# Three heads of an HGRN2 mixer project two token blocks by Strassen's seven products, and the mixers' outputs pass through DRAM

## The chip, the cores and the metric

The kernel runs on one core of one Trainium2 chip. Its time is the device time of an execution in microseconds, as the median of several runs. TensorE (PE) multiplies into PSUM banks, its matmuls preceded by loads of weights (PEld); VectorE (DVE), ScalarE (ACT) and GpSimd (POOL) do the element-wise work; DMAs are issued from SyncE's queue (SP). Each engine works through its own queue in order and waits at an instruction whose operands or buffers are not ready.

## What is computed

One inference step of a hybrid layer on 1056 tokens (1024 of a prompt, 32 of eight running sequences), all in float32 with a width of 1024. Cut to what matters:

```python
h = _rmsnorm(x, norm_mix)
p = jnp.einsum('btd,dp->btp', h, w_in) + b_in
qk_a, v_a, o_a, i_a, f_a, q_b, f_b, i_b, g_b = jnp.split(p, offs, axis=-1)
out_a = _mlstm_mixer(...)            # 4 heads of 128
out_b = _hgrn_mixer(q_b, f_b, i_b, g_b, S0, lb, hgrn_norm)   # 4 heads of 128
#   f = lb + (1 - lb) * sigmoid(f_raw);  k = (1 - lb) * sigmoid(-f_raw);  q = silu(q_raw)
#   chunks of 64: gated linear attention with a state S;  out = headnorm(o) * silu(g_raw)
x = x + concat([out_a, out_b]) @ w_out
h2 = _rmsnorm(x, norm_ffn)
x = x + (silu(h2 @ w_gate) * (h2 @ w_up)) @ w_down
```

The states of both mixers are outputs too.

## The kernel before, in words

Everything lies transposed: features on the 128 partitions, tokens along a row. The tokens form three blocks: block 0 of 288 (256 of the prompt and the 32 samples), blocks 1 and 2 of 384. A float32 operand is split into a rounded part (HI, whi) and the rest (LO, wlo), both in a format that TensorE multiplies fast, and a product is three matmuls: hi x hi, hi x lo, lo x hi (lines 135 to 137). ScalarE makes the rounded part and GpSimd the rest (lines 96 and 97).

The work is a list of units, in the order of TensorE. A unit is one weight tile (128 outputs by 1024 inputs) against one block: 8 steps along the inputs of 3 matmuls, 24 in all, into a PSUM bank, which an evacuation then empties. First come the four heads of the mLSTM mixer, then from unit 51 the four heads of HGRN2, each with tiles for f, q, v and g and three blocks, so 12 units a head; then the output projection and the feed-forward part, which already works by Strassen's scheme.

Between the matmuls of a unit stand hooks, one after every 6 matmuls. At a hook each active generator takes its next step: the mixers (`mix_b` for HGRN2), the splitting of weight tiles (`split`), the norms. A mixer of one head and block takes some 32 hooks, so two or three overlap: products of 16 or 32 columns on TensorE (line 775), merging by masked copies (line 782), state updates (line 899), steps that multiply halves of the queries and keys by gates (lines 794, 796 and 802) with copies on ScalarE (lines 799 and 800), the gate product of a new mixer on GpSimd (line 804). Its result goes into X in place (line 928), in the place that the normalised input has left.

Weight tiles come through two raw buffers; when a tile is split, the load for the tile after next is issued. `next_splits` starts a split eight units ahead of the first use, or as soon as one of five split buffers is free. The projections' banks come from three buffers named mm; the evacuations are lines 472 and 474 (v, q, g) and 741 to 744 (f and the key made of it). On SP's queue the DMAs stand in the order in which they were written.

Of the kernel before, what the change touches and what calls it, by code (L numbers as in the profile page):

```python
# [16 lines left out]
T = 1056  # L17
# [23 lines left out]
def hybrid_step(ctx: ExitStack, tc: tile.TileContext, i, o):  # L41
# [13 lines left out]
    units, tiles = [], []  # L55
# [30 lines left out]
    def split(t, pool):  # L86
# [11 lines left out]
        if t < NRAW:  # L98
            load(t + 4)
        elif 4 <= t and t + NRAW < len(tiles) and (t + NRAW < n_t1) == (t < n_t1):  # L100
            load(t + NRAW)
# [19 lines left out]
    def unit(t, rhs, nk, evac, stride=128, coff=0, post=None, tag="mm"):  # L121
        units.append(dict(t=t, rhs=rhs, nk=nk, evac=evac, stride=stride, coff=coff, post=post, tag=tag))

    def emit_k(u, ks):
# [3 lines left out]
        if ks[0] == 0:  # L128
            u["ps"] = bank(u["tag"])
        ps = u["ps"]  # L130
        hi, lo = his[t], los[t]
        for k in ks:
            c = k * u["stride"] + u["coff"]
            wh, wl = hi[:, c:c + 128], lo[:, c:c + 128]
            nc.tensor.matmul(ps[:, :n], wh, rh[:, k, :], start=(k == 0), stop=False)  # L135
            nc.tensor.matmul(ps[:, :n], wh, rl[:, k, :], start=False, stop=False)  # L136
            nc.tensor.matmul(ps[:, :n], wl, rh[:, k, :], start=False, stop=(k == nk - 1))  # L137
# [24 lines left out]
    def mo(b):  # L162
        return X[:, :, PO[b]:PO[b] + NPR[b]]
# [74 lines left out]
    def tl(tag, n=384, bufs=2, dt=F32, p=128):  # L238
        return mp.tile([p, n], dt, tag=tag, name=tag, bufs=bufs)
# [34 lines left out]
    d_x = dram.tile([128, KT, T], F32, name="d_x")  # L274
    d_h = dram.tile([128, KT, T], F32, name="d_h")
# [12 lines left out]
    def gates(ps, b):  # L288
# [8 lines left out]
        else:  # L297
            A, B, Cc = (mp.tile([36, 384], F32, tag=x, name=x) for x in ("gA", "gB", "gC"))
            me = mp.tile([4, 385], F32, tag="gm", name="gm")
# [104 lines left out]
    def conv_evac(kind, h, b):  # L404
        j = h if kind == "q" else 4 + h

        def ev(ps):
# [5 lines left out]
            if acc is None:  # L413
                acc = tl("c" + kind, 384, 1 if kind == "q" else 2)
# [68 lines left out]
    def load_bc(h, b):  # L483
        ng, wi = tl("ngb", 384, 1), tl("wib", 388, 2)
# [21 lines left out]
    def mix_a(h, b):  # L506
# [79 lines left out]
        for c in range(ncb):  # L586
# [3 lines left out]
        nc.vector.scalar_tensor_tensor(mo(b)[:, h, :], pH[:, :npr], col(V_MN + h), S["o", h, b][:, :npr],  # L590
                                       op0=OP.mult, op1=OP.mult)
# [144 lines left out]
    def f_evac(h, b):  # L736
        def ev(ps):
            n = BL[b]
            f, k = tl("ngb", 384, 1), tl("ck", 384, 2)
            S["f", h, b], S["kb", h, b] = f, k  # L740
            nc.scalar.activation(f[:, :n], ps[:, :n], AF.Sigmoid, bias=col(V_BIN + 20 + h))
            nc.scalar.activation(k[:, :n], ps[:, :n], AF.Sigmoid, bias=nbf[:, h:h + 1], scale=-1.0)
# [4 lines left out]
    def mix_b(h, b):  # L747
# [159 lines left out]
        for c in range(ncb):  # L907
            s = slice(c * 128, c * 128 + 128)
            nc.tensor.matmul(pO[:, s], AT[:, c, :], vt[:, s], start=True, stop=cin[c] is None)
            if cin[c] is not None:  # L910
                nc.tensor.matmul(pO[:, s], qp[:, s], cin[c], start=False, stop=True)
# [1046 lines left out]
```

## Time and profile before

| | |
| --- | --- |
| three runs | 1389.91, 1391.82, 1394.54 us; median 1391.82 |
| the profiled execution | 1394.97 us, of which 1392.9 us lie between its first and its last instruction |
| mean granted clock of TensorE | 0.982 |
| mLSTM stage, 130 to 260 us | TensorE busy 128.42 of 130 us |
| HGRN2 head 1, head 2 | 63.6 us each |
| head 1: busy PE, DVE, ACT, POOL | 63.26, 33.58, 25.59, 15.69 us |

In the profile's rows a line such as `390.50 0.58 ACT L472 ACTIVATE cq<-mm,vec` gives the start, the duration, the engine, the line of the kernel, the operation and the tiles written and read; in square brackets stands how long the engine was idle before it, and what it waited for. A stage's row gives the busy time of each engine with its count of instructions, then the granted clock of TensorE, the share of the DMA engines' time and GB/s. A row of waits gives the total, the count and the longest. In a group's row the number after the bar is the busy time of the group, then the mean duration in ns of one instruction. Line numbers are those of the kernel before; the changed kernel's are higher, and its lines are named where they are shown.

### The profile page before, as it was taken

Reading aid. Unit: us, or ns where it says so; the run is one execution under the profiler, and the core shown is the slowest. Engines: PE = TensorE matmul, PEld = TensorE weight load, DVE = VectorE, ACT = ScalarE, POOL = GpSimd, SP = SyncE. Lnnn points to the kernel's source line nnn. Section 1 sums busy time; section 2 is a strip of 40 time slices with the busy share of each in tenths; the row PEclk is TensorE's granted clock in tenths of the full one; section 3 lists DMA queues with packets and bytes.
Section 4 is the critical chain, followed back from the end, with each engine's and each line's share of the span. In section 5 each row is a group of like instructions: output and inputs, shape, how many; then the busy total and the mean of one; then the engine's idle time right before and its main releaser. Section 6 shows DMA issues by size and latency. Waiting matters only on the chain.

```text
span 1392.9 us, 29377 instructions
## 1 busy us (share of the span) xinstructions
PE 1337.1 (96%) x11600; PEld 1306.0 (94%) x11600; DVE 868.0 (62%) x2060; ACT 558.6 (40%) x1315; POOL 593.3 (43%) x566
## 2 busy tenths in 40 slices
PE   7888999999999999999998999999999999999996
PEld 7778999899999998999998999999999999999995
DVE  7876667664555456644666667666765346777765
ACT  6554434233344334422435445554544341222232
POOL 5223212231222213222437666666666683444434
PEclk9999999999999999999999999999999999999997
DMA  6012122230101013553464666567654278878743
GB/s 226 23 38 60 66 63 74 87 109 17 49 32 49 32 49 116 149 160 109 163 202 171 211 227 250 204 216 254 218 210 168 78 261 321 300 278 295 278 152 125
DMA packets 108881, 212.11 MB, mean 152 GB/s; under 512 B 10800, under 2 KB 63560, under 8 KB 108232
## 3 DMA queue, kind: packets, MB, share of 16 engines
q1 hardware_dynamic: 108312, 209.98, 43.9%
q8 instruction: 91, 1.49, 0.4%
q14 instruction: 46, 0.38, 0.1%
q10 hardware_dynamic: 432, 0.27, 0.1%
HBM read 143.76 MB, written 66.45 MB: 151 GB/s over the span
## 4 chain that ended last, share of the span: by engine, by line
PE 78%; DVE 10%; ACT 4%; DMA 3%; issue 3%; SPq 1%; POOL 0%; POOLq 0%; DVEq 0%; ACTq 0%
PE mx L1260 16%; PE mm L135 9%; PE mm L1260 9%; PE mm L137 9%; PE mm L136 9%; PE mx L1483 8%; PE mm L1483 5%; PE so L1260 3%; PE mx L644 1%; PE mx L775 1%; PE so L1483 1%; DMA rg<-d_ff 1%; ACT HI L229 1%; DVE X L228 1%; DMA X<-d_x 1%
## 5 line engine op out<-in xcount | busy, mean ns | idle before, releaser
L135 PE MATMUL mm<-HI,whi 128*128 128x384 f32 (+2 forms) x1160 | 379.3, 327 | 6.6 <-ACT gA L302 2.9
L137 PE MATMUL mm<-HI,wlo 128*128 128x384 f32 (+2 forms) x1160 | 363.5, 313 | 1.1 <-POOL wlo L97 1.1
L136 PE MATMUL mm<-LO,whi 128*128 128x384 f32 (+2 forms) x1160 | 363.1, 313 | 0.4 <-POOL LO L225 0.2
L135 PEld LDWEIGHTS mm<-HI,whi 128*128 128x128 f32 x1160 | 221.4, 191 | 11.8 <-ACT gA L302 3.2
L137 PEld LDWEIGHTS mm<-HI,wlo 128*128 128x128 f32 x1160 | 221.3, 191 | 1.6 <-POOL wlo L97 1.6
L136 PEld LDWEIGHTS mm<-LO,whi 128*128 128x128 f32 x1160 | 221.7, 191 | 1.1 <-POOL LO L225 0.5
L97 POOL TENSOR_TENSOR wlo<-raw,whi 128x512 fp32r<-128x512 f32 x90 | 118.6, 1328 | 216.1 <-ACT whi L96 171.1
L1189 POOL TENSOR_TENSOR wlo<-S,whi 128x512 fp32r<-128x512 f32 x78 | 110.3, 1420 | 88.2 <-ACT whi L1188 85.2
L1260 PE MATMUL mx<-T,whi 128*128 128x264 f32 x640 | 118.2, 284 | 0.0
L1260 PEld LDWEIGHTS mx<-T,whi 128*128 128x128 f32 x640 | 99.0, 188 | 0.0
L1313 POOL TENSOR_TENSOR LO<-rg,HI 128x528 fp32r<-128x528 f32 x52 | 70.6, 1369 | 65.1 <-ACT HI L1312 65.1
L1260 PE MATMUL mx<-HI,whi 128*128 128x264 f32 x320 | 91.0, 285 | 0.0
L1260 PE MATMUL mx<-HI,wlo 128*128 128x264 f32 x320 | 90.9, 284 | 0.0
L1260 PE MATMUL mx<-T,wlo 128*128 128x264 f32 x320 | 90.9, 284 | 0.0
L1260 PE MATMUL mx<-LO,whi 128*128 128x264 f32 x320 | 90.7, 283 | 0.0
L1401 DVE TENSOR_TENSOR fh<-fr,fh 128x512 fp32r<-128x512 f32 x80 | 66.2, 828 | 35.0 <-ACT fh L1396 34.7
L1487 DVE TENSOR_TENSOR X<-X,mx 128x264 f32<-128x264 f32 x160 | 65.6, 425 | 26.5 <-PE mx L1483 25.9
L1188 ACT ACTIVATE whi<-S 128x512 fp32r<-128x512 f32 x80 | 50.3, 630 | 71.4 <-DVE S L1177 71.3
L1312 ACT ACTIVATE HI<-rg 128x528 fp32r<-128x528 f32 x52 | 32.3, 641 | 104.5 <-PE mx L1483 28.3
L1260 PE MATMUL mm<-HI,wlo 128*128 128x264 f32 x240 | 68.2, 284 | 0.0
L1260 PE MATMUL mm<-HI,whi 128*128 128x264 f32 x240 | 68.2, 284 | 0.0
L1260 PE MATMUL mm<-LO,whi 128*128 128x264 f32 x240 | 67.9, 283 | 0.0
(545 smaller groups left out, 3424.1 us busy)
## 6 DMA issues: line engine op xcount, KB each, us to landing
d_wf<-fh SPq DMA_DIRECT2D x60, 512.0 KB
rg<-d_ff SPq DMA_DIRECT2D x42, 528.0 KB
raw<-in_wA SPq DMA_DIRECT2D x31, 512.0 KB
whi<-d_wf SPq DMA_DIRECT2D x29, 512.0 KB
wlo<-d_wf SPq DMA_DIRECT2D x28, 512.0 KB
raw<-in_wgu SPq DMA_DIRECT2D x24, 512.0 KB
d_ff<-sg SPq DMA_DIRECT2D x40, 264.0 KB
rg<-in_wgu SPq DMA_DIRECT2D x20, 512.0 KB
```

Of the source, the lines that this page charges most:

```text
L97: (nc.gpsimd if pool else nc.vector).tensor_tensor(lo[:, s], raw[:, s], hi[:, s].bitcast(F32), op=OP.subtract)
L135: nc.tensor.matmul(ps[:, :n], wh, rh[:, k, :], start=(k == 0), stop=False)
L136: nc.tensor.matmul(ps[:, :n], wh, rl[:, k, :], start=False, stop=False)
L137: nc.tensor.matmul(ps[:, :n], wl, rh[:, k, :], start=False, stop=(k == nk - 1))
L1188: nc.scalar.activation(hi[:, s], t, AF.Copy)
L1189: (nc.vector if dve else nc.gpsimd).tensor_tensor(lo[:, s], t, hi[:, s].bitcast(F32), op=OP.subtract)
L1260: nc.tensor.matmul(ps[:, :QN], a[:, w], b_[:, kk, c], start=new and kk == 0 and x == 0, stop=kk == 3 and x == 2, skip_group_check=True)
L1312: nc.scalar.activation(h, src, AF.Copy)
L1313: (nc.vector if dve else nc.gpsimd).tensor_tensor(lw, src, h.bitcast(F32), op=OP.subtract)
L1401: nc.vector.tensor_tensor(lw, src, h.bitcast(F32), op=OP.subtract)
L1483: nc.tensor.matmul(ps[:, :QN], a[:, w], b_[k][:, cs], start=new and k == 0 and x == 0, stop=k == 1 and x == 2, skip_group_check=True)
L1487: nc.vector.tensor_tensor(y, y, ps[:, :QN], op=OP.add)
```

## The change

**Seven products.** For heads 0, 1 and 2 of HGRN2 the tiles are taken in pairs, (f, q) and (v, g). The two tiles, each cut into two halves of 512 inputs, are A11, A12 (first tile) and A21, A22 (second); the normalised blocks 1 and 2, cut in the same way, are B11, B21 (block 1) and B12, B22 (block 2). Instead of four units of 24 matmuls, seven of 12 are made: P1 = A11 B11, P2 = A12 B21, P5 = S1 T1, P6 = S2 T2, P3 = S4 B22, P7 = S3 T3, P4 = A22 T4, in this order, three of them adding on in P1's bank. Block 0's units stand between: one ahead of P4, one behind it. Head 3 stays as it was.

**Weight sums.** `pairs_split` forms S1 to S4 in place in the two raw tiles with four sums on VectorE and rounds each half tile (line 134 after, the rest on GpSimd at 135). Two empty entries in the list of tiles hold the results; the loads of the next pair's tiles are written behind the last of these roundings, since they go into the same raw buffers, and the next pair's first tile is split from that hook on.

**Block sums.** After the first norm, blocks 1 and 2 are also stored to DRAM (`d_n`). During the last mLSTM units `x1_prep` fetches them piece by piece and makes T1, T2 and T4 with their roundings; they lie in X's place (`TX`) and in a small extra tile. `x3_prep` makes T3 in the place of B12, which is saved in DRAM (`d_b`) and brought back behind the last P7.

**Mixer outputs.** As X's place is taken, the outputs go to DRAM (`d_m`) two hooks after they are made (`mixed`), and `x_back` fetches them into a new X behind the last P4; the last head's three and two of the head before it are written into it directly.

**Evacuations.** The banks of the projections from unit 51 are three fixed ones (`pm`). P2's is copied by ScalarE, then VectorE adds P1's bank to it (line 1145 after); P5 and P6 are copied, P3 and P7 added; the sigmoids of f, q and g of block 2 come afterwards, those of f at the start of its mixer. Some buffers get a second or third copy (ngb, cq, v, go); the mixers start at other hooks, and wait at three places for the mixer before.

Cut to its core, the diff reads:

```diff
+    def pairs_split(tb, ta, raw_a, raw_b):
+        while ("w", raw_b) not in done:
+            yield 1
+        ra, rb = raws[raw_a], raws[raw_b]
+        a11, a12, a21, a22 = ra[:, 0:512], ra[:, 512:1024], rb[:, 0:512], rb[:, 512:1024]
+        def rnd(t, s, src):
...
+            nc.scalar.activation(his[t][:, s], src, AF.Copy)
+            nc.gpsimd.tensor_tensor(los[t][:, s], src, his[t][:, s].bitcast(F32), op=OP.subtract)
+        left, right = slice(0, 512), slice(512, 1024)
+        nc.vector.tensor_tensor(a22, a21, a22, op=OP.add)
+        yield 1
+        rnd(tb, right, a22)
+        done.add(("S1", tb))
+        nc.vector.tensor_tensor(a21, a11, a21, op=OP.subtract)
+        nc.vector.tensor_tensor(a11, a22, a11, op=OP.subtract)
+        yield 1
+        rnd(ta, left, a11)
+        done.add(("S2", tb))
+        nc.vector.tensor_tensor(a12, a12, a11, op=OP.subtract)
+        yield 1
+        rnd(ta, right, a12)
+        done.add(("S4", tb))
+        yield 1
+        rnd(tb, left, a21)
+        done.add(("S3", tb))
+        for x in nexts.get(ta, ()):
+            load(x)
...
+    def mixed(m, b, ps, gain, gate):
+        n = NPR[b]
+        direct = m == KT - 1 or m == KT - 2 and b
+        nc.vector.scalar_tensor_tensor(mo(b)[:, m, :] if direct else gate[:, :n], ps, gain, gate[:, :n], op0=OP.mult, op1=OP.mult)
+        if not direct:
+            yield 2
+            nc.sync.dma_start(d_m[:, m, PO[b]:PO[b] + n], gate[:, :n])
+        done.add(("mixed", m, b))
...
+        def add(name, b, ps):
+            t = S[name, h, b]
+            nc.vector.tensor_tensor(t, t, ps[:, :384], op=OP.add)
...
+        def p2(ps):
+            put(n0, 1, ps)
+            add(n0, 1, pm[0])
...
+    XF = {"P1": (0, 0, "B11"), "P2": (0, 512, "B21"), "P3": (3, 512, "B22"), "P4": (1, 512, "T4"), "P5": (2, 512, "T1"),
+          "P6": (3, 0, "T2"), "P7": (2, 0, "T3")}
...
+        for p, bk in (("P1", 0), ("P2", 1), ("P5", 2), ("P6", 0), ("P3", 2), ("P7", 0), ("P4", 0)):
+            if p == "P4":
+                mid()
+            d_, coff, b_ = XF[p]
+            need = {"P5": "S1", "P6": "S2", "P3": "S4", "P7": "S3"}.get(p)
+            unit(ta + d_, (Op(b_, 0), Op(b_, 1)), 4, evs[p], coff=coff, post=posts.get(p), need=need and (need, ta + 2),
+                 bank=pmb(bk), acc=p in ("P6", "P3", "P7", "P4"))
```

**Where it moves instructions.** ScalarE in the HGRN2 stage before, from the evacuation of an f unit (ngb) to that of a v unit: the roundings of weights (whi<-raw) stand singly between evacuations (from the banks mm) and the mixers' copies.

```order
L741 ACTIVATE ngb<-mm,vec 128x384
L742 ACTIVATE ck<-mm,nbf 128x384
L799 ACTIVATE qB<-qw 128x6x32
L800 ACTIVATE kB<-ck 128x6x32
L96 ACTIVATE whi<-raw 128x512
L863 ACTIVATE AT_121<-mx 32x3x32 x2
L864 ACTIVATE AT_121<-mx 64x3x64
L96 ACTIVATE whi<-raw 128x512
L472 ACTIVATE cq<-mm,vec 128x384
L879 ACTIVATE vt<-mx 128x384
L96 ACTIVATE whi<-raw 128x512 x2
L472 ACTIVATE v<-mm,vec 128x384
```

ScalarE now, around the first products of the f and q pair of a head: the two L134 rows below are the roundings of S4 and S3, L519 is the evacuation of q of block 0, L904 a mixer's copy.

```order
L519 ACTIVATE cq<-mm,vec 128x288
L904 ACTIVATE AT_124<-AD_126 32x3x32 x4
L134 ACTIVATE whi<-raw 128x512
L859 ACTIVATE qB<-qw 128x6x32
L860 ACTIVATE kB<-ck 128x6x32
L134 ACTIVATE whi<-raw 128x512
L96 ACTIVATE whi<-raw 128x512 x2
L1139 ACTIVATE ngb<-mm 128x384
L923 ACTIVATE AT_124<-mx 32x3x32 x2
L924 ACTIVATE AT_124<-mx 64x3x64
```

The two L96 rows round the next pair's first tile, whose load is written behind S3's rounding; P2's evacuation (L1139) and the mixer's copies now stand behind them.

GpSimd before, in the same stage: L97 are the subtractions for weight tiles, L804 the gate product with which a mixer starts, L498 a power in its norm.

```order
L97 TENSOR_TENSOR wlo<-raw,whi 128x512 x3
L498 TENSOR_TENSOR sm<-sm,mhalf 128x3
L97 TENSOR_TENSOR wlo<-raw,whi 128x512
L804 TENSOR_TENSOR qw<-cq,ngb 128x288
L498 TENSOR_TENSOR sm<-sm,mhalf 128x3
```

GpSimd now, at the place of ScalarE's rows: L135 are the subtractions for S1 to S4, L97 those for the next pair's tiles, L864 the gate product of the next head's block 0.

```order
L135 TENSOR_TENSOR wlo<-raw,whi 128x512
L545 TENSOR_TENSOR sm<-sm,mhalf 128x3
L135 TENSOR_TENSOR wlo<-raw,whi 128x512 x3
L97 TENSOR_TENSOR wlo<-raw,whi 128x512 x2
L864 TENSOR_TENSOR qw<-cq,ngb 128x288
L97 TENSOR_TENSOR wlo<-raw,whi 128x512 x2
```

Four subtractions have come in, and the gate product of block 0 stands behind two that use a tile whose load is written only behind S3.

280 lines of the change are left out of this document (234 added, 46 removed).

## The prediction, made before the changed kernel ran

> **What bounds the kernel now.** I read the page first, then the busy time by stage, then what TensorE waits for in the HGRN2 stages.
>
> ```profile
> span 1392.9 us, 29377 instructions
> ...
> PE 1337.1 (96%) x11600; PEld 1306.0 (94%) x11600; DVE 868.0 (62%) x2060; ACT 558.6 (40%) x1315; POOL 593.3 (43%) x566
> ...
> core 0: us, PE busy (x) PEld busy (x) DVE busy (x) ACT busy (x) POOL busy (x), PEclk, DMA share, GB/s
> ...
> 365.00:428.60 63.60, 63.26 (x815) 60.01 (x814) 33.58 (x124) 25.59 (x82) 15.69 (x16) 1.00 0.11 36
> 428.60:492.20 63.60, 63.26 (x814) 60.01 (x813) 33.55 (x124) 25.59 (x81) 15.66 (x16) 1.00 0.11 36
> ```
>
> The two windows are heads 1 and 2 of HGRN2. TensorE is busy 63.26 of 63.60 us, at the full granted clock; the other engines are half idle and DMA nearly so. So a matmul removed here is time removed, and any new wait of TensorE is time added. The waits of TensorE from 296 to 560 us show how little there is now:
>
> ```profile
> PE mx L858 <- DVE wib L802: 2.0, 4, 1.4
> PE so L672 <- DMA st<-in_S: 1.5, 2, 1.3
> PE mx L775 <- DVE wib L802: 0.9, 1, 0.9
> PE mx L694 <- DVE sjunk L691: 0.6, 1, 0.6
> ```
>
> In the middle heads that is one wait of 0.2 us each. Matmuls overlap, so their worth is the distance from start to start, not their duration. Ten starts lie between the first two rows, 22 between the other two:
>
> ```profile
> 550.34 0.34 PE L136 MATMUL mm<-LO,whi 128*128 128x384 f32 x1
> ...
> 552.08 0.34 PE L137 MATMUL mm<-HI,wlo 128*128 128x384 f32 x1
> ...
> 363.51 0.29 PE L136 MATMUL mm<-LO,whi 128*128 128x288 f32 x1
> ...
> 366.44 0.29 PE L137 MATMUL mm<-HI,wlo 128*128 128x288 f32 x1
> ```
>
> That is 0.174 us for a matmul of 384 columns and 0.133 us for one of 288.
>
> **What is removed.** In each of three heads, two pairs of weight tiles against two blocks took 2 x 4 x 24 = 192 matmuls of 384 columns; seven products of 12, twice, are 168. The program has 72 fewer of them: 72 x 0.174 = 12.5 us, all on the path.
>
> **What is added off the path.** Per head ScalarE gets 8 roundings and 4 evacuations or sigmoids more, VectorE 8 weight sums and 6 additions, GpSimd 8 subtractions. By the rows below that is about 7, 10 and 10 us per head beside half-idle engines. The block sums (16 on each of the three engines) lie under the last mLSTM units; the copies through DRAM (normalised blocks, the covered operand, mixer outputs) are some 17 MB over the whole stretch, where the DMA share is 0.11 in the rows above. I cost all that at nothing by itself; if the cover were gone, the load of a few microseconds at the head of a queue would show. What costs is the order.
>
> **What is added on the path: a weight load that a queue waits for.** Today a weight tile is loaded six units ahead of its rounding, some 30 us (12 units take 63.6). Now the four sums are made in the two raw tiles, and the next pair's two loads go into these tiles, so a load starts only when GpSimd has read the last sum; the rounding that waits for it is written into ScalarE's queue right behind. Queued behind it are the mixer's copies and the evacuation of P2, whose addition on VectorE frees the bank that P6 needs; on GpSimd the next mixer's gate product stands behind two subtractions that wait for the same load. The durations:
>
> ```profile
> 378.07 0.28 ACT L916 ACTIVATE kt<-mx 128x128 f32<-128x128 f32 x1 [1.98 <-PE mx L911]
> ...
> 378.75 0.21 ACT L916 ACTIVATION_READ_ACCUMULATOR kt<-mx 128x1 f32 x1
> ...
> 383.26 1.05 ACT L844 ACTIVATE AT<-AD 32x64 f32<-32x64 f32 x4 [1.55 <-DVE AD L782]
> 384.32 0.63 ACT L96 ACTIVATE whi<-raw 128x512 fp32r<-128x512 f32 x1
> ...
> 390.50 0.58 ACT L472 ACTIVATE cq<-mm,vec 128x384 f32<-128x384 f32 x1 [1.91 <-PE mm L137]
> 391.12 0.62 DVE L474 SCALAR_TENSOR_TENSOR cq<-mm,vec,cq 128x384 f32<-128x384 f32 x1 [2.62 <-ACT cq L472]
> ...
> L899 DVE SCALAR_TENSOR_TENSOR C<-C,wib,mx 128x128 f32<-128x128 f32 x22 | 7.6, 346 | 0.7
> L796 DVE TENSOR_TENSOR kB<-ck,wib 128x192 f32<-128x192 f32 x14 | 5.0, 354 | 0.0
> L1177 DVE TENSOR_TENSOR S<-raw 128x512 f32<-128x512 f32 x18 | 13.4, 745 | 0.0
> ...
> 371.14 0.81 POOL L804 TENSOR_TENSOR qw<-cq,ngb 128x288 f32<-128x288 f32 x1 [9.63 <-DVE cq L474]
> 379.31 0.85 POOL L498 TENSOR_TENSOR sm<-sm,mhalf 128x3 f32<-128x3 f32 x1 [7.36 <-DVE AD L782]
> 385.03 1.29 POOL L97 TENSOR_TENSOR wlo<-raw,whi 128x512 fp32r<-128x512 f32 x1 [1.97 <-ACT whi L96]
> ```
>
> A 512 KB weight load alone is issued at 449.95 and has moved by 452.7, 2.8 us:
>
> ```profile
> 449.95 0.33 SPq L107 DMA_DIRECT2D raw<-in_wA  x1
> ...
> 451.50:452.00 0.50, 0.50 (x3) 0.50 (x4) 0.46 (x3) 0.48 (x3) 0.00 (x0) 1.00 0.96 393
> 452.00:452.50 0.50, 0.50 (x4) 0.50 (x4) 0.10 (x2) 0.20 (x1) 0.00 (x0) 1.00 0.92 377
> 452.50:453.00 0.50, 0.50 (x6) 0.47 (x4) 0.00 (x0) 0.00 (x0) 0.00 (x0) 1.00 0.20 74
> ```
>
> Let T be the first matmul of a pair's P1. P4 of the pair before ended about 4.3 us earlier (24 x 0.133 and a mixer's matmuls). **First kind: the f and q pairs of heads 1 and 2.** VectorE comes out of P4's evacuation, three state updates and two mixer steps (starts about 0.27 apart) at T - 0.5; three sums bring it to T + 1.7. ScalarE then rounds S1, squares the mixer's output (0.9), rounds S2, evacuates q, copies AT (1.05) and rounds S4 by T + 4.75; GpSimd subtracts until T + 6.05. The load lands at T + 8.9, two roundings end at T + 10, P2's evacuation and addition at T + 11.1. P6 would be due at T + 7.8 (36 matmuls, 6.3, and 1.5 of mixers): 3.3 us. On GpSimd two subtractions from T + 9.5 and the gate product end at T + 12.9; the products that need it are due at T + 7.4: 5.5 us. If VectorE is done with the sums before its mixer steps delay them, S4 is subtracted by T + 3.9 and the same chain gives 3.4 us. I take 4.5, between these. **Second kind: the v and g pairs of heads 0 to 2.** There GpSimd's gate product stands ahead, and S4 follows the sums at once: subtracted by T + 3.7, loaded by T + 6.5, P2 added by T + 8.9 against T + 7.9; the state updates that stand behind that addition hold the mixer's output products until T + 9.5 against 7.6. I take 2.0, bounds 0 (the load lands 1 us earlier and VectorE is free) and 3.5 (two mixer steps late as well).
>
> | term | us | bounds |
> | --- | --- | --- |
> | 72 matmuls | -12.5 | -12.5 |
> | 2 pairs of the first kind x 4.5 | +9.0 | +5 to +13 |
> | 3 pairs of the second kind x 2.0 | +6.0 | 0 to +10.5 |
> | three mixer steps with no projection between, before the last head's units | +0.7 | 0 to +2 |
> | the last mixer before the output projection, one step later | +1.3 | 0 to +2 |
> | denser mixers, block sums, start | +0.5 | -1 to +3 |
> | sum | +5.0 | -8.5 to +18 |
>
> The first bound of each kind leaves 2.5 and 0; the two steps are bounded by the L858 waits above (up to 1.4) and by this row, in which the output projection now waits 0.36 for a split that will stand one step later, behind 0.61 of VectorE and 0.64 of ScalarE:
>
> ```profile
> 669.44 0.39 PE L135 MATMUL mm<-HI,whi 128*128 128x264 f32 x1 [0.36 <-DVE X L1010]
> ```
>
> The start could gain or lose: the gate rows' broadcast loads get a second buffer, and two 768 KB stores stand ahead of them on SP; I put both near nothing. After the output projection the program is the same, and TensorE bounds it, so nothing given up here is won back. The profiled execution took 1394.97 us for its span of 1392.9; with +5.0 it would be about 1400.0. The median before is 1391.82, 3.15 lower, so the median after is forecast at 1396.8.
>
> **A rule about waits.** The stage at 540 to 570, with waits of up to 1.4 us, ran at 0.97 of the clock:
>
> ```profile
> 540.00:570.00 30.00, 26.52 (x356) 22.74 (x355) 20.41 (x56) 15.36 (x44) 15.37 (x23) 0.97 0.64 182
> ```
>
> The Trainium skill, "TensorE: Matmul & The Clock Gate", Part 1, says that an idle window of about 3.4 us halves the clock until TensorE has been busy as long. By that rule each wait of the first kind could cost up to 1.7 us more, an estimate from that page, and the sum would be +8.4, within the forecast's own range and part of its chance; no wait in this stage of the trace is that long, so no run here shows it yet.
>
> **The rivals.** *The loads are early enough (faster, 0.20).* If VectorE and ScalarE run ahead, S4 is subtracted about T + 2 instead of T + 6: the load lands at T + 5, P2 is added by T + 7.2, before P6 is due, and only the gate product of the first kind waits, some 1.5 us, twice. With 1.5 for the rest the sum is -12.5 + 3 + 1.5 = -8: 1384. For it: ScalarE waits for TensorE in nearly all its gaps today. Against it: S4 stands behind an evacuation that can't start before T. It decides when S4 is subtracted before T + 3. *Gain and waits cancel (same, 0.34).* The lower chain for the first kind (3.4) and 1.2 for the second with 2 for the rest gives 12.4 against 12.5: 1392. *VectorE and GpSimd block each other (slower, 0.11).* A step of 0.35 took 1.36 beside a subtraction of GpSimd:
>
> ```profile
> 350.85 2.52 POOL L97 TENSOR_TENSOR wlo<-raw,whi 128x512 fp32r<-128x512 f32 x2
> ...
> 352.23 1.36 DVE L794 TENSOR_TENSOR qw<-qw,ngb 128x192 f32<-128x192 f32 x1
> ```
>
> With such a delay of 1.0 in two of the four sums of each of five pairs the sum is +15: 1407. The Trainium skill, "SBUF — State Buffer", section "Who interferes with whom", says that a VectorE instruction with two SBUF inputs waits for a GpSimd instruction that reads SBUF, for the whole of it; these rows agree (1.36 against 0.35). That the program doesn't do what it says is no rival: its order holds 1512 matmuls of 384 columns where 1584 stood.
>
> **How the numbers follow.** A measurement of this kernel tells about 0.3% (4.2 us) from no change. The forecast itself, some +4 to +11, has 0.35; VectorE and GpSimd in each other's way 0.11; so slower 0.46, same 0.34, faster 0.20. The range reaches to the first rival's time below and to between the forecast and the blocked case above: 1384 to 1405. Its likeliest part alone, the forecast's own, is 1395 to 1403.
>
> **What would show it.** In the profile after: 72 fewer matmuls at the projections' lines; ScalarE's rounding of the raw tiles ending gaps of 2 to 5 us released by the load of raw, five times, while TensorE waits at P6 for VectorE's addition or, at the next head's first mixer products, for GpSimd's gate product; heads 0 to 2 as long as before within 3 us. I am wrong if TensorE stays at 99% there (then the loads were early), if it waits for the sums' roundings themselves at P5 or P3, or if the loss stands in the start or behind the output projection.

## The result, and the profile after

Four runs of the changed kernel took 1431.96 to 1436.38 us, median 1435.12; four of the kernel before, beside them, 1389.91 to 1394.70, median 1393.18. The ratio is 1.0301, 95% interval 1.0273 to 1.0328: the change costs 42 us, where +5 was forecast. The profiled execution took 1431.96 us, the shortest of the four, with a span of 1430.1; the spans of the two profiles differ by 37.2 us, and it is these that are told apart below.

The page after, in the order of the rows shown of before: span, busy engines, the clock granted to TensorE in 40 slices, and the shares of the chain that ended last.

```profile
span 1430.1 us, 29548 instructions
...
PE 1339.4 (94%) x11528; PEld 1303.9 (91%) x11528; DVE 936.2 (65%) x2118; ACT 585.9 (41%) x1367; POOL 646.8 (45%) x606
...
PEclk7999999899999999999999999999999999999997
...
PE 69%; DVE 16%; ACT 5%; issue 4%; DMA 3%; POOL 2%; SPq 0%; POOLq 0%; DVEq 0%; ACTq 0%
```

TensorE is busy 2 us longer in all, with 72 matmuls fewer: what is left of the answer must be waits and a lower clock. To find where, the starts of the units were set side by side. Unit 39 starts at 228.2 us before and at 227.1 after. From there two stretches grow: units 39 to 45 (the last mLSTM head, where the block sums are made), and the heads of HGRN2, from the third unit of HGRN2 to the first unit of the output projection. The two stretches, of before and then of after:

```profile
228.20:257.60 29.40, 27.82 (x211) 27.07 (x211) 22.25 (x78) 10.59 (x35) 7.46 (x18) 1.00 0.31 93
306.80:558.60 251.80, 246.33 (x3154) 230.89 (x3153) 136.98 (x493) 100.50 (x311) 64.64 (x77) 1.00 0.15 48
```

```profile
227.10:271.70 44.60, 33.18 (x211) 31.27 (x210) 28.70 (x89) 14.43 (x44) 16.72 (x27) 0.85 0.32 103
320.80:593.90 273.10, 244.89 (x3082) 227.18 (x3081) 191.40 (x543) 123.27 (x357) 103.54 (x105) 0.95 0.23 76
```

The first grew by 15.2 us, the second by 21.3. With -1.1 us ahead of them, -0.1 between them and +1.9 behind that is the 37.2 us between the two spans. In the heads VectorE is busy 54 us longer and GpSimd 39. In both stretches the granted clock, the number after the five engines, fell from 1.00 to 0.85 and 0.95.

**The heads.** What TensorE waits for there (total, times, longest):

```profile
PE mx L953 <- DVE kt L944: 7.2, 3, 2.5
PE mx L918 <- DVE wib L862: 6.8, 3, 2.8
PE mx L740 <- DVE sjunk L737: 3.7, 1, 3.7
PE mx L913 <- DVE ck L856: 3.5, 2, 1.7
PE mx L937 <- DVE kB L856: 2.7, 3, 1.3
```

With the smaller ones it is 28.0 us, all but 0.2 for VectorE, against 5.0 before. So the stretch is 251.8 - 12.5 (the 72 matmuls) + 23.0 = 262.3 us by the waits, and the other 10.8 us of 273.1 are put down to the clock: of the 27.3 us in which it was granted by half, TensorE was busy for 22.7, half of which is 11.3. By units, 16.2 us of the waits stand in the middle of P2 of five pairs, 3.3 to 3.4 us after a pair's first matmul, and 3.7 in the first pair's P1. This is VectorE at the f and q pair of head 1, whose P1 starts at 386.4 (that is T of the prediction), then GpSimd, TensorE and ScalarE there, and the row of the stretch at half clock that begins within TensorE's second wait:

```profile
385.06 0.68 DVE L137 TENSOR_TENSOR raw<-raw 128x512 f32<-128x512 f32 x1
385.78 0.69 DVE L141 TENSOR_TENSOR raw<-raw 128x512 f32<-128x512 f32 x1
386.51 0.69 DVE L142 TENSOR_TENSOR raw<-raw 128x512 f32<-128x512 f32 x1
387.21 1.17 DVE L540 TENSOR_SCALAR sm<-sm 128x3 f32<-128x3 f32 x1
388.29 0.68 DVE L146 TENSOR_TENSOR raw<-raw 128x512 f32<-128x512 f32 x1
388.89 0.51 DVE L521 SCALAR_TENSOR_TENSOR cq<-mm,vec,cq 128x288 f32<-128x288 f32 x1
...
389.67 1.46 DVE L854 TENSOR_TENSOR qw<-qw,wib 128x192 f32<-128x192 f32 x1
391.05 0.34 DVE L856 TENSOR_TENSOR ck<-ck,wib 128x192 f32<-128x192 f32 x1
...
392.18 0.98 DVE L854 TENSOR_TENSOR qB<-qw,wib 128x192 f32<-128x192 f32 x1
393.08 1.41 DVE L856 TENSOR_TENSOR kB<-ck,wib 128x192 f32<-128x192 f32 x1
```

```profile
386.55 1.80 POOL L135 TENSOR_TENSOR wlo<-raw,whi 128x512 fp32r<-128x512 f32 x1 [13.97 <-issue]
...
389.65 1.26 POOL L135 TENSOR_TENSOR wlo<-raw,whi 128x512 fp32r<-128x512 f32 x1
391.67 2.60 POOL L135 TENSOR_TENSOR wlo<-raw,whi 128x512 fp32r<-128x512 f32 x2 [0.76 <-ACT whi L134]
...
391.45 0.38 PE L913 MATMUL mx<-qw,ck 128*32 128x32 f32 x12 [1.73 <-DVE ck L856]
394.63 0.85 PE L918 MATMUL mx<-qB,kB 128*32 128x64 f32 x12 [2.80 <-DVE wib L862]
...
396.17 1.15 ACT L96 ACTIVATE whi<-raw 128x512 fp32r<-128x512 f32 x2 [3.55 <-DMA raw<-in_wA]
```

```profile
393.30:400.10 6.80, 5.47 (x27) 5.00 (x27) 3.10 (x5) 2.85 (x7) 4.20 (x4) 0.50 0.50 157
```

VectorE has the four sums ahead of a mixer's steps L854 and L856, and three of these steps take 0.98 to 1.46 us instead of 0.34, each beside one of GpSimd's remainders of a sum (L135). TensorE, with 12 matmuls in P1 and 6 of P2 ahead of them, waits 1.73 and 2.80 us for them, and the clock is halved for 6.8 us, 5.5 of which lie behind the second wait. ScalarE's wait for the raw tile, on which the forecast rested, is there too, with 3.55 us; it ends 1.5 us after TensorE's second wait.

**Units 39 to 45.** TensorE's waits, and then SyncE's queue and the instruction that it held up:

```profile
PE mx L619 <- DVE C L604: 4.4, 1, 4.4
PE mx L617 <- DVE PB L767: 3.2, 1, 3.2
PE mx L596 <- POOL vt L586: 2.5, 1, 2.5
PE mx L760 <- DVE kt L588: 1.3, 1, 1.3
```

```profile
235.01 0.43 SPq L1082 DMA_DIRECT2D kB<-d_n  x1
...
244.58 0.32 SPq L1082 DMA_DIRECT2D qB<-d_n  x1
...
250.82 0.42 SPq L1082 DMA_DIRECT2D kB<-d_n  x1
251.30 0.42 SPq L754 DMA_DIRECT2D ngS<-d_bc  x1
...
255.04 0.43 SPq L757 DMA_DIRECT2D nT<-in_n0T  x1
...
256.85 0.25 DVE L763 SCALAR_TENSOR_TENSOR sW<-ngS,scol,cst 128x32 f32<-128x32 f32 x1 [5.70 <-DMA nT<-in_n0T]
```

The last round of the block sums' loads (L1082) waits for its buffers until 250.82, mostly because the round before is still being summed. The sample step's loads (L754 to L757) stand right behind in the same queue; VectorE waits 5.70 us for the last of them, and TensorE twice for VectorE. TensorE's waits here are 11.4 us against 1.6 before, so 9.8 of the 15.2 us; the other 5.4 are put down to the clock, which was halved for 13.7 us.

### The profile page after: what moved, and what is told of

Read it like the earlier page. It is cut to its first block, busy times and chain, and to the rows that moved or that the text cites. A ratio compares the mean times of both kernels' runs of the same rounds, so it can differ in the third digit from the quotient of the medians.

```text
span 1430.1 us, 29548 instructions
## 1 busy us (share of the span) xinstructions
PE 1339.4 (94%) x11528; PEld 1303.9 (91%) x11528; DVE 936.2 (65%) x2118; ACT 585.9 (41%) x1367; POOL 646.8 (45%) x606
## 4 chain that ended last, share of the span: by engine, by line
PE 69%; DVE 16%; ACT 5%; issue 4%; DMA 3%; POOL 2%; SPq 0%; POOLq 0%; DVEq 0%; ACTq 0%
PE mx L1513 15%; PE mm L1513 9%; PE mm L168 8%; PE mm L169 7%; PE mm L170 7%; PE mx L1736 7%; PE mm L1736 4%; PE so L1513 3%; DMA rg<-d_ff 1%; PE mx L690 1%; PE mx L835 1%; ACT HI L272 1%; DVE X L271 1%; PE so L1736 1%; PE mm L1777 1%
## 5 line engine op out<-in xcount | busy, mean ns | idle before, releaser
L168 PE MATMUL mm<-HI,whi 128*128 128x384 f32 (+2 forms) x1064 | 348.5, 328 | 5.7 <-ACT qB L349 2.9
L170 PE MATMUL mm<-HI,wlo 128*128 128x384 f32 (+2 forms) x1064 | 334.4, 314 | 1.3 <-POOL wlo L97 1.3
L169 PE MATMUL mm<-LO,whi 128*128 128x384 f32 (+2 forms) x1064 | 334.4, 314 | 0.6 <-DVE LO L1246 0.3
L168 PEld LDWEIGHTS mm<-HI,whi 128*128 128x128 f32 x1064 | 206.1, 194 | 10.7 <-ACT qB L349 3.2
L170 PEld LDWEIGHTS mm<-HI,wlo 128*128 128x128 f32 x1064 | 206.2, 194 | 1.8 <-POOL wlo L97 1.8
L169 PEld LDWEIGHTS mm<-LO,whi 128*128 128x128 f32 x1064 | 206.4, 194 | 1.4 <-DVE LO L1246 0.6
L97 POOL TENSOR_TENSOR wlo<-raw,whi 128x512 fp32r<-128x512 f32 x90 | 118.9, 1332 | 179.0 <-ACT whi L96 146.5
```

Source lines behind the costliest of these rows:

```text
L97: (nc.gpsimd if pool else nc.vector).tensor_tensor(lo[:, s], raw[:, s], hi[:, s].bitcast(F32), op=OP.subtract)
L168: nc.tensor.matmul(ps[:, :n], wh, rh[:, k, :], start=(k == 0 and not u["acc"]), stop=False, skip_group_check=sk)
```

## The experiments

The theories, by the letters used in what was expected. **L**: the forecast's, the late raw load. **V1**: VectorE's four sums stand in the mixers' chain at P1 and P2. **V2**: GpSimd's remainders of the sums lengthen VectorE's steps in that chain. **Q**: SyncE's queue ahead of HGRN2; **D**: there the sums' work itself. Times are medians, ratios are to before on the same chip; 1.0301 is the change as it is.

### One cause at a time in the heads

**No reload of the raw tiles** (in `pairs_split`):

```diff
-        for x in nexts.get(ta, ()):
-            load(x)
+        for x, r in zip(nexts.get(ta, ()), (raw_a, raw_b)):
+            raws[x] = raws[r]
```

> The raw tiles of the next pair are not loaded after the sums of the pair before: its roundings take what lies in the two buffers. It leaves out ten loads of 512 KB, so five pairs are projected with the wrong weights; the instructions on the engines are the same. Forecast's theory L (the load that can't start before the sums are rounded sets the end): its two terms, 9 + 6 us, go and with them some of the clock's loss: 1412 to 1424 us. Theory V (VectorE's and GpSimd's work stands in the mixers' chain, the load is waited for by ScalarE alone): no wait of TensorE goes, 1431 to 1437 us.

Measured: 1423.08 us, 1.0202 (1.0185 to 1.0220), within L's band. But TensorE's waits at P2 stood as they were (4.5, 4.5 and three of 2.3 to 2.5 us). The heads took 265.2 us: the first pair's wait fell from 3.7 to 0.8, those at P5 (0.3 and 1.1) went, and the half-speed clock of the heads fell from 27.3 to 17.1 us. The loads matter, then, but not through the wait that the forecast named.

**No weight sums**: VectorE's four `tensor_tensor` of `pairs_split` left out.

> VectorE's four subtractions and additions of each pair of weight tiles are left out, so four of the seven products take plain quarters of the weights in place of sums; the roundings of ScalarE and GpSimd stay. Theory V1 (VectorE's own added work, 24 times 0.69 us and what they queue behind, delays the mixers' chain at P2): TensorE's waits of 2.3 to 4.5 us at P2 shrink by most of the 2.8 us that four sums take: 8 to 14 us come off, with the clock's part: 1421 to 1427 us. Theory V2 (GpSimd's twice as many remainders of 1.3 us block VectorE's two-input instructions, which stand at 1.3 to 1.5 us in place of 0.35): these long instructions stay, 2 to 6 us come off: 1429 to 1433 us. Theory L: nothing, or 2 to 4 us since the roundings and with them the loads start earlier.

Measured: 1418.41 us, 1.0162 (1.0141 to 1.0184), more than V1 expected. The waits of the v and g pairs at P2 are gone; those of the f and q pairs fell from 4.5 to 2.9. The heads:

```profile
318.70:577.80 259.10, 241.04 (x3081) 223.61 (x3081) 169.85 (x522) 121.86 (x356) 99.42 (x104) 0.97 0.24 79
```

**No remainders of the sums on GpSimd** (the rounding's second half left out, `los[t] = los[raw_b if t == tb else raw_a]`):

> GpSimd's 24 remainders of the weight sums are left out (the products take the plain quarters' remainders), VectorE's sums and ScalarE's roundings stay. Theory V2 (VectorE's two-input instructions stand behind GpSimd's running one): VectorE's mixer steps at P1 and P2 go back to 0.35 us, 2 to 4 us a pair in the chain: 7 to 14 us come off, 1421 to 1428 us. Theory V1 (the sums' own time in VectorE's queue): the 2.3 us waits at P2 of the v and g pairs stay, at most 4 us come off: 1431 us or more. Theory L: the next load starts up to 5 us earlier in each pair, since it waits for the last remainder, 2 to 5 us.

Measured: 1423.06 us, 1.0208 (1.0191 to 1.0224): V2's band as well, with waits of 0.8 us at most left at the v and g pairs; two of 3.8 and 4.0 come up at P5 of the f and q pairs, of which more below.

```profile
319.00:583.40 264.40, 242.08 (x3083) 223.91 (x3081) 173.61 (x540) 122.50 (x356) 75.38 (x84) 0.97 0.24 78
```

So V1 and V2 are each right in part: taking either away takes most of the waits at P2 away. In the heads 9 of the mixer steps L854, L856 and L862 took over 0.8 us before, 29 after, 27 without the sums and 17 without the remainders.

**The remainders on VectorE** (`nc.vector` for `nc.gpsimd` in `rnd`), and **in pieces of 256 columns**:

> The 24 remainders of the weight sums (the second half of each rounding) are made by VectorE and not by GpSimd; all else stays. Theory V2 (GpSimd blocks VectorE): VectorE's mixer steps at the pairs go back from 1.3 to 1.5 us to 0.35, two or three of them a pair in the chain, while 4 remainders of some 0.6 us are added a pair: 3 to 10 us come off: 1425 to 1432 us. Theory V1 (VectorE's amount of work): 24 times 0.6 = 14 us more on the engine that is waited for, 4 to 12 us more: 1439 to 1447 us. Theory L: the roundings end earlier by up to 0.7 us each, 2 to 5 us come off.

> GpSimd's remainders, those of the weight sums and of the plain tiles of HGRN2 and the output projection, are made in pieces of 256 columns, twice as many of half the length; all else stays. Theory V2 (a two-input instruction of VectorE waits for the end of GpSimd's running one): VectorE's mixer steps at the pairs fall from 1.3 to 1.5 us to some 0.7, two or three a pair: 3 to 8 us come off: 1427 to 1432 us. Theory V1 alone (the sums' own time): no gain, 1433 to 1440 us, since GpSimd gets 60 instructions more. Theory L: no gain.

Measured: 1437.53 us, 1.0313 (1.0294 to 1.0332), and 1434.65 us, 1.0296 (1.0281 to 1.0312). The first lies between V2's band and V1's: on VectorE the remainders cost as much by their own time as they had by blocking it, and the heads took 280.1 us. The pieces gain nothing, against V2's forecast: more steps meet a piece. At head 1 three steps in a row take 0.77, 0.88 and 0.68 us, where two of them took 0.98 and 1.41 and the third 0.15, and in all the heads 31 still take over 0.8.

**No weight work at all**: neither sums nor their roundings; the products take the plain tiles, and the next raw tiles are loaded as soon as these are rounded.

```diff
...
+        for t, r in ((tb, raw_b), (ta, raw_a)):
+            his[t], los[t] = his[r], los[r]
+        done.update(("S%d" % k, tb) for k in (1, 2, 3, 4))
```

> No weight sums, roundings or remainders of sums at all: the sum tiles are the plain tiles themselves, and the next raw tiles are loaded as soon as the plain ones are rounded. The 72 matmuls fewer, the order of the units and the sums put together behind the products stay. If the weights' work is what costs (V1, V2 and L together), the heads take before's 251.8 us less 12.5, some 240 us in place of after's 273, with less than 7 us of waits: 1398 to 1406 us. Rival S (the half units of 12 matmuls and three mixer steps with no projection between them leave the mixers' chain without cover): the heads stay above 250 us, 1411 us or more.

Measured: 1407.79 us, 1.0095 (1.0080 to 1.0109), just above the first band. The heads:

```profile
321.60:568.00 246.40, 234.15 (x3083) 217.63 (x3081) 154.69 (x514) 109.74 (x324) 71.73 (x83) 1.00 0.25 83
```

Against 273.1 the weight work, with the late loads that it causes, costs 26.7 us of the heads. Of the 12.5 us that the fewer matmuls are worth 5.4 show; the other 7 are 6.3 us of waits more than before, which the half units leave (theory S in part).

**Plain heads**: no products and no weight sums, but block sums, outputs by way of DRAM and larger pools kept. T3 is made one unit after HGRN2 begins.

> Heads 0 to 2 of HGRN2 are projected plainly as before, 24 matmuls a unit, with no weight sums; the block sums are still made (units 33 to 51), and so are the mixer outputs' way by DRAM, the x_back loads and the larger pools. Block 2 then reads its own second half where the sum T3 was put, so its values are others'. Theory by stage (queue Q ahead of HGRN2, VectorE's and GpSimd's weight work V in it, the DRAM route free): units 39 to 45 keep their 15 us, the heads go back to before's 251.8 us within 3: 1409 to 1417 us. Rival M (the route of the mixer outputs by DRAM and the new order of the mixer steps cost in the heads too): 1420 us or more. Rival N (nothing is lost ahead of HGRN2 that the heads wouldn't have hidden): 1400 us or less.

Measured: 1416.87 us, 1.0163 (1.0143 to 1.0183). The heads took 251.80 us, as before to the last digit:

```profile
327.20:579.00 251.80, 247.21 (x3168) 230.66 (x3168) 133.62 (x486) 101.00 (x313) 67.29 (x80) 1.00 0.22 75
```

The mixer outputs' way through DRAM and the larger pools cost nothing there. The two units of HGRN2 ahead of this stretch, where T3 is now made, took 18.2 us in place of 10 and are not in the 251.8: TensorE waits 3.7 us there for the same step (L737) as in the first pair's P1 of the changed kernel, 1.3 us for another, and 6.8 us run at half clock. For that step the run settles nothing.

### Two limits, one behind the other

**Weight sums ahead**: the four sums in a generator of their own, started with the second plain tile's rounding.

```diff
+    def pairs_sums(raw_a, raw_b):
+        while ("w", raw_b) not in done:
+            yield 1
...
+            yield 2
+            nc.vector.tensor_tensor(o_, a, b, op=op)
...
-        while ("w", raw_b) not in done:
+        while ("ws", raw_b) not in done:
```

> The four sums of a pair of weight tiles are written right behind the rounding of the pair's second plain tile, two hooks apart, some 20 us ahead of where they stand; the roundings stay, since they wait for a tile buffer. Theory V1 (the sums stand in the mixers' chain at P1 and P2, where TensorE has half a unit of work): where they now stand TensorE waits for nothing, so nearly all that leaving them out gave comes here too: 1420 to 1427 us, and the waits of 2.3 to 2.5 us at P2 of the v and g pairs go. Rival (VectorE is over 70% busy all through the heads, so its amount of work counts, not the place): at most 4 us come off, 1431 us or more. Theory L (the raw loads): the sums' roundings end up to 2 us earlier, 2 to 5 us come off.

Measured: 1429.89 us, 1.0254 (1.0237 to 1.0272), well short of V1. The waits at P2 went (4.5 to 0.9, 2.3 to 0), and new ones came at P5 and P6. At the same pair of head 1:

```profile
395.79 0.63 ACT L96 ACTIVATE whi<-raw 128x512 fp32r<-128x512 f32 x1 [4.24 <-DMA raw<-in_wA]
396.32 0.47 ACT L1144 ACTIVATE ngb<-mm 128x384 f32<-128x384 f32 x1
...
396.83 0.56 DVE L1150 TENSOR_TENSOR ngb<-ngb,mm 128x384 f32<-128x384 f32 x1 [4.25 <-ACT ngb L1144]
397.30 0.68 DVE L859 TENSOR_TENSOR qB<-qB,wib 128x192 f32<-128x192 f32 x1
...
398.39 0.30 PE L942 MATMUL mx<-ident,kB 128*128 128x128 f32 x1 [3.71 <-DVE kB L861]
```

This is the forecast's chain: ScalarE waits for the raw load, P2's evacuation stands behind it, VectorE's addition waits for that, and TensorE for what is behind the addition, a mixer's step and not P6. In the changed kernel the sums hid it; at the same place stand the 3.8 and 4.0 us of the run without remainders.

**The late rounding of the raw tiles**, alone and with the sums ahead:

```diff
     def split(t, pool):
+        late = t not in raws
         while t not in raws or (t and t - 1 not in his):
             yield 1
+        if late:
+            yield 6
```

> Only the late rounding of the raw tiles, with the weight sums where the change has them. Theory V+L: TensorE's waits at P2 (2.3 to 4.5 us) stay, since the sums and remainders set them; the first pair's 3.7 us and the 0.3 to 1.1 us at P5 go, as without the loads at all: 1422 to 1428 us. Forecast's theory L (the load is what costs): its 15 us and the clock's part, 1412 to 1420 us. Rival V1 alone: 1432 to 1437 us.

> The weight sums ahead as in the run before, and ScalarE's rounding of a raw tile that was loaded behind the sums is written six hooks later, behind the evacuations of the pair's first products. In the run with the sums ahead alone ScalarE waits 4.2 and 4.5 us for that load with an evacuation behind it, and TensorE 3.7 us for VectorE's mixer step behind that. Theory V+L (two limits, one behind the other: the sums first, the load next; either alone gives little): now both go: the waits at P5 of 1.4 to 3.7 us and the first pair's 4.3 us go, 15 us with the clock's part, so 1412 to 1420 us. Rival V1 alone (the sums set the end and the load is waited for by ScalarE alone): no more than the 1430 us of the sums ahead. Rival (VectorE and GpSimd are short of time as a whole): 1425 us or more, with waits at other mixer steps.

Measured: alone 1437.11 us, 1.0312 (1.0294 to 1.0329), no gain, where V+L had 1422 to 1428, since the waits at P2 stay and three of 1.4 to 1.7 us join them; both together 1417.40 us, 1.0177 (1.0154 to 1.0200), within the band of V+L. The first gives 5 us, the second none, the two 18. The waits that are left, three of 2.9 us, stand at the v and g pairs, where the late remainders of the plain tiles now lie: two mixer steps beside them take 0.96 and 1.14 us.

### Ahead of HGRN2

**Block sums twelve units earlier** (`first_b - 30` for `first_b - 18`):

> The block sums start twelve units earlier (30 units ahead of HGRN2 and not 18), so their loads on SyncE's queue no longer stand ahead of the loads of the last mLSTM head's sample step. Theory Q (the queue): in the changed kernel units 39 to 45 lose 15.2 us to TensorE of before because SyncE waits 13 us for the sums' buffers with the sample step's loads behind it; that goes, so 12 to 15 us come off 1435: 1420 to 1423 us, and unit 51 starts within 2 us of before's 296.8. Rival D (density: there is simply more work for VectorE and GpSimd under the mLSTM units): the loss moves to the units where the sums now are, at most 4 us come off: 1431 us or more. The forecast's theory (the waits for the raw tiles in HGRN2) says nothing of this stage: no change.

Measured: 1422.61 us, 1.0206 (1.0189 to 1.0223). This is within Q's band. Units 39 to 45 took 29.4 us, as before; but units 21 to 33 lost 5 us, where TensorE now waits 2.5 us for GpSimd's copy L586, and runs at half clock for 3.4.

**The sample step's loads from ScalarE**, alone, and with sums ahead and late rounding:

> The block sums stay where the change has them, but the sample step's loads are issued by ScalarE and not by SyncE. Theory Q (SyncE waits 13 us for the sums' buffers with these loads behind it): three of TensorE's four waits in units 39 to 45, 8.8 us, go, and most of the half clock that follows them: 9 to 13 us come off: 1422 to 1426 us; the wait of 2.5 us for GpSimd's copy stays. Rival D (the sums' work itself is too much for VectorE and GpSimd there): at most 4 us come off: 1431 us or more.

> Weight sums ahead, late rounding of the raw tiles, and the sample step's loads issued by ScalarE. The block sums stay under the last mLSTM head, where they cost units 21 to 33 nothing. If the stages add: the 18 us of the first two and the 9 to 13 of the third, 1404 to 1410 us. If the clock or VectorE takes part of it back, as with the early block sums: 1411 to 1417 us.

Measured: 1443.60 us, 1.0351 (1.0336 to 1.0366), and 1434.49 us, 1.0292 (1.0265 to 1.0318): worse. ScalarE came to these loads at 250.13, hardly earlier than SyncE (251.30), as its queue holds the roundings of the block sums; the later loads of the sample steps then stood behind its evacuations, which cost 7 us in units 45 to 51 and 9 in the output projection. This told nothing of Q.

**The sample step's loads first** in SyncE's queue (the fourth round of `x1_prep` waits until they are written), with sums ahead and late rounding:

> Weight sums ahead and late rounding as before, the block sums where the change has them, but the loads of their fourth and last round are written behind the sample step's loads on SyncE's queue; the work is the same. Theory Q (the sample step's loads stand behind SyncE's wait for the sums' buffers): they are issued some 10 us earlier, TensorE's three waits of 8.8 us go: 8 to 12 us under the 1417 us of the run without: 1405 to 1409 us. Rival D (the sums' work on VectorE, ScalarE and GpSimd delays the sample step itself): at most 4 us come off, 1413 us or more, and the waits stand elsewhere.

Measured: 1414.99 us, 1.0149 (1.0127 to 1.0172). The loads are issued 15 us earlier, with the sums' last round behind them:

```profile
236.52 0.43 SPq L763 DMA_DIRECT2D ngS<-d_bc  x1
...
240.34 0.43 SPq L766 DMA_DIRECT2D nT<-in_n0T  x1
...
248.47 0.32 SPq L1093 DMA_DIRECT2D qB<-d_n  x1
```

```profile
226.70:262.60 35.90, 29.96 (x211) 28.66 (x211) 26.99 (x87) 13.86 (x43) 15.63 (x26) 0.95 0.41 126
```

The stretch takes 35.9 us in place of 44.6, or of 42.7 in the run that lacks this edit alone, and the wait of 3.2 is gone, that of 4.4 down to 2.0. So by the traces 6.8 to 8.7 us of the stretch are the queue (Q); the 6.5 us over before's 29.4 that stay are left to the sums' work on GpSimd and VectorE (D) and the clock. The time is in D's band and not in Q's: by the medians only 2.4 us of the gain show against the run without, and the two intervals overlap.

### Put together

> Block sums twelve units earlier, weight sums behind the plain rounding and remainders of 256 columns, together. If the three act in different places their gains add: 12.5 us for the block sums as measured, 8 to 14 for the weight sums, 3 to 8 for the pieces, and 3 to 6 of the clock's half-speed stretches: 1400 to 1412 us. If the mixers' chain is short of VectorE time anyway, or the raw loads take over as what is waited for, 1412 to 1420 us. Under before's 1394 only if all waits of the heads went, which no theory says: the first head's start (3.7 us) and the last mixers stay.

> The run with the sums ahead and the late rounding, and the block sums twelve units earlier too. The block sums stand in another stage, so their gain adds in full: 12 us under the run without, 1400 to 1408 us by theory V+L; 1410 to 1420 us if VectorE and GpSimd are short of time as a whole. Before's 1394 would be reached only if the clock's half-speed stretches of the heads went with the waits (27 us of them after, which cost 11.5 us).

> Weight sums ahead and late rounding as before, and the block sums six units earlier (24 ahead of HGRN2), so that their last loads stand some entries ahead of the sample step's on SyncE's queue and not right before them. If the sums collide with the sample step alone: TensorE's three waits of 8.8 us in units 39 to 45 go with the half clock behind them, 8 to 12 us under the 1417 us of the run at 18 units: 1405 to 1409 us. If, as twelve units earlier, part of it comes back where the sums now are (5 to 7 us there, GpSimd's copy waited for): 1411 to 1415 us.

Measured: 1426.65 us, 1.0229 (1.0202 to 1.0257); 1414.26 us, 1.0149 (1.0129 to 1.0169); 1414.76 us, 1.0148 (1.0134 to 1.0162). The first is above both its bands: it lacks the late rounding, and the raw load is waited for as with the sums ahead alone. The other two are in their upper bands, so the gains of the stages don't add in full. The best versions are some 20 us slower than before, half of the change's loss. The heads of the second took 259.3 us, 7.5 more than before. None of these points to a version faster than before.

## Why the prediction was wrong

**The 72 matmuls, -12.5: right.** 1512 matmuls of 384 columns stand where 1584 stood; without the weight work 5.4 us of it show in the heads' length, and 6.3 us of added waits account for most of the rest.

**The raw load, +9.0 and +6.0: the mechanism is there, and it was not what cost.** ScalarE's rounding of a raw tile ends five gaps of 1.8 to 3.6 us released by the load in the five pairs meant, as the prediction said. But TensorE did not wait behind them at P6, and for the next gate product it waited 0.2 us in all: it had waited before, at P2. The step that failed is the one that cost the sums and their remainders "at nothing by itself", and with it the path: the prediction followed P2's addition and the next gate product and never asked when the running mixer's own steps, which stand behind the sums in VectorE's queue, would be done; TensorE came for them after 18 matmuls, at T + 3.3. The sums themselves were not late. By the rows of head 1 the third ends at T + 0.8, where the prediction had T + 1.7, and the fourth at T + 2.6; but the mixer steps behind them end at T + 8.1, since three of them meet a remainder of GpSimd. Without the loads the heads are still 18.8 us longer than without any weight work, so sums, roundings and remainders are the greater part of the 26.7 us, in that order of removal. Only with the sums or the remainders out of the way did the forecast's chain set the end, with 3.7 to 4.0 us.

**The size of these terms was met by luck.** The waits at P2 are 4.5 us in each pair of the first kind and 2.3 to 2.5 in the second, 16.2 in all where 15.0 stood in the sum; but they stand at another place and have another cause. A sixth gap of ScalarE, 3.98 us to 317.75 and ahead of the first pair, was not priced: evacuations stand behind it, VectorE waits 5.23 us for them, and the first pair's 3.7 us at P1 fall to 0.8 when the loads are left out.

**Where the 32.2 us between +5.0 and the profiles' 37.2 lie.** The waits of the heads came to 23.0 us where 15.7 were priced (+7.3), the clock there to 10.8 where nothing stood, the stretches ahead of the heads to 14.0 where 0.5 stood (+13.5), and what follows the heads to 1.9 where 1.3 stood (+0.6).

**The third rival was the nearest.** VectorE and GpSimd in each other's way had 0.11 and +15. What it priced, two of four sums longer by 1.0, came in the three v and g pairs: the first sum took 1.50 us beside the gate product on GpSimd, and the third or fourth 1.67 to 1.82 beside a remainder, where 0.68 and 0.69 are usual. In the f and q pairs no sum was longer; there the mixer's steps behind the sums were, which it left out. The row quoted for it (1.36 against 0.35) was the right one.

**Denser mixers, block sums and start, +0.5 with bounds -1 to +3: far off, +14.** The start gave up nothing (-1.1). The block sums were taken as work under the last mLSTM units; their loads were not followed through SyncE's queue, though the prediction spoke of "the load at the head of a queue". What was queued behind them, the sample step's loads, is what it should have named.

**The clock: left out of the sum, with +3.4 as an estimate beside it.** 27.3 us of the heads and 13.7 of units 39 to 45 ran at half clock, 10.8 and 5.4 us by the workings above. The Trainium skill, "TensorE: Matmul & The Clock Gate", Part 1, says that the gate looks at free-running windows of 3.4 us; the stretches at half clock here are 3.4, 6.8 and 10.2 us long, which agrees. Read as a rule on waits as long as 3.4 us, as the prediction did, it was too mild: waits of 2.3 to 2.8 us were enough in some places. The profile of before had a case already: the row quoted for 540 to 570 us holds not only waits of up to 1.4 us but one of 1.97, up to 567.9, and 3.4 us at half clock from 568.5 on.

**The two small steps at the end, +0.7 and +1.3.** The first, three mixer steps with no projection between, is at 522 to 526 us, within the heads: TensorE waits 0.91, 0.87 and 0.40 us there, 2.2 in all, just above its bound of 2, and 3.4 us at half clock follow. The second belongs to the output projection, which took 0.6 us more, with no half clock where before had 3.4 us of it; another 1.3 us came in the feed-forward part, where the program is the same. The total of 1.9 behind the heads is near 1.3 without its parts being shown.

**What stays open.** The causes don't add: without sums the heads gain 14.0 us, without remainders 8.7, without loads 7.9, together 30.6 against the 26.7 of all weight work, and the late rounding gives nothing alone. How much is each one's has no answer but the order in which they are removed. That the early block sums gave 12.5 us alone but 3.1 on top of the sums ahead and the late rounding is not explained; the spans of those two profiled executions differ by 11.8.

## What to carry to other kernels

Work put beside half-idle engines is free only if it doesn't stand ahead of the steps that the bounding engine waits for next: at each place where work is added, list what is queued behind it on that engine and when that is due, above all where the bounding engine's own work has been cut. Follow each DMA that waits for a buffer to the DMAs behind it in its queue. When one removed limit gives little, look for the next in the same chain before giving it up: here two edits that gave 5 us and nothing gave 18 together.

## What the hardware showed

In these heads the clock cost about half as much again as the waits: 23.0 us of added waits, 10.8 us of clock. It is not a matter of one wait's length alone. Two waits of 2.3 us at the same place of heads 1 and 2 end at 428.8 and 498.5; the rows of the stretches behind them show the granted clock at 0.51 behind the second and at 1.00 behind the first:

```profile
499.10:502.50 3.40, 3.40 (x58) 3.32 (x57) 1.07 (x1) 1.41 (x3) 2.14 (x2) 0.51 0.68 183
428.80:432.20 3.40, 3.40 (x65) 3.25 (x66) 1.59 (x3) 1.64 (x4) 2.08 (x2) 1.00 0.62 195
```

What differs is where they lie. In this trace the changes of the granted clock all stand on one grid with steps of 3.41 us; 427.46 and 495.73 are points of it:

```profile
424.05:427.46 3.41, 2.39 (x14) 2.07 (x12) 3.38 (x6) 1.33 (x4) 3.41 (x4) 1.00 0.00 0
427.46:430.88 3.42, 2.12 (x57) 2.00 (x58) 2.94 (x7) 1.37 (x4) 1.89 (x4) 1.00 0.49 158
495.73:499.14 3.41, 1.09 (x7) 0.69 (x5) 3.38 (x10) 1.28 (x4) 2.47 (x5) 1.00 0.23 60
```

The first wait lies across a point of the grid and leaves TensorE idle for 1.0 and 1.3 us of two steps; the second lies within one step, 2.3 us of it idle, and the next step runs at half clock. The run with the sums ahead has the same with waits of 3.7 us: the one that ends at 398.4 is parted into 1.9 and 1.8 us and no half clock follows, the one that ends at 466.0 leaves 2.6 us of one step idle and 6.8 us at half clock follow. In the changed kernel's heads all six full-clock steps with 1.5 us or more of idle time were followed by half clock, and none with 1.3 or less was; as the 1.9 of the other run shows, that is no fixed threshold.
